# First layer of a two-layer trunk: parameter loads put ahead of four weight loads, parameters transposed 65 products earlier, one exponential on 64 values

## The chip, the cores and the metric

The kernel runs on one core of a Trainium2 chip. TensorE (PE) multiplies, VectorE (DVE), ScalarE (ACT) and GpSimd (POOL) work on tiles beside it, and SyncE (SP) issues the DMAs. The metric is the device time of one execution in microseconds, as the median of three runs. Beside it there is one profiled execution with its trace.

## What is computed

Two layers follow one another. Each projects 256 rows of 2048 columns to queries, keys, values and the input `u` of a state-space part, mixes them, multiplies by `w_out`, normalizes, and runs an MLP of 8192 columns. Cut to what matters here:

```
for l in range(2):
    proj = x @ w_in[l]                      # q, k, v, u: 1024 columns each
    attn_out = diff_attention(q, k, v, ...)  # 8 heads, softmax over allowed keys
    dt = exp(ssm_log_dt)[:, None]            # 64 groups: 64 different values
    mag = exp(lam_re * dt)                   # 64 groups x 64 states
    a   = mag * (cos(lam_im * dt), sin(lam_im * dt))
    f   = (a - 1) / lam                      # complex
    bb  = f * b                              # h[t] = a h[t-1] + bb u[t];  y = Re(c h) + d u
    ssm_out = norm(glu(gelu(y)))
    x = layer_norm(ALPHA * x + concat(attn_out, ssm_out) @ w_out[l])
    x = layer_norm(ALPHA * x + relu(x @ w_up[l])**2 @ w_down[l])
```

## The kernel before

**Products.** Every large product is made of matmuls of 128x128 by 128x512 (L202, called products below). A float32 factor is split into a high and a low part, and three products (high by high, high by low, low by high) stand for one. Weights come in tiles `w` of 256 rows by 512 columns (512 KB). For each, SP issues one DMA (L180, `wpair`), ACT copies the high part `wh` (L155), and DVE subtracts to get the low part `wl` (L136). Six tiles `w` and four pairs `wh`, `wl` can be held at once. A group of 256 rows x 512 columns of output is 96 products (16 blocks of 128 rows by 2 halves by 3). In each layer the mixer has eight such groups of the input projection: keys (first half), two of `u`, queries, two of values, keys, queries. Then 96 products with the first half of the attention output follow, which are ready early. That makes 864 products; what comes then needs the end of the state-space part or of the attention.

**State-space part.** Its parameters are loaded by `load_params`, a generator that SP's order follows: `prm` (32x128 twice), `ld` (the 64 values of `ssm_log_dt`), `vec`, `lb` (two tiles, 64-byte pieces), `lc` (c_re and c_im, two DMAs each, 256-byte pieces) and `lq` (four broadcasts). `lay_params` turns them: PE transposes `prm` and `vec` to `prmT_ps`, then `lc` in four groups of four. POOL takes two powers of e (`ex` for dt, `mag`), each 128x32. DVE makes the angles `ang`, ACT takes sine and cosine `pw`, and DVE forms `ab`, `f` and `base`. Then POOL makes `abc`, `fine` and the table `tab` (`half_prep`, `ssm_prep`). After that the part runs in eight blocks b0 to b7 of 128 channels. Each block has two groups of small matmuls `X` (L540, 8 each), which DVE multiplies with `tab`, scans, and multiplies again (tiles `wk`), and then a group `Y` (L572, L581), followed by a gelu on DVE and ACT.

**Attention.** Each of eight heads has scores `S`, a softmax on DVE and ACT (tiles `pe`), a transpose and a product `pT`, a norm with a power `ss` on POOL, and a transpose of `o`.

**What sets the order.** SP and PE run in the order in which the program emits its steps. In the mixer that order comes from `Flow`, a planner with a clock of its own (`fl.now`): each step is given a due time with constants such as `L_LOAD` and `L_PARAM`, and a step with a lower priority number is taken first once it is due. The constants only place instructions; the chip's waits are on semaphores. DVE, ACT and POOL are ordered by a scheduler from the same emission. A DMA of SP waits for the one eight places before it.

In the first layer the loop in `main` over the first product calls the parameter loads: five steps of the generator at the fourth of its steps (i == 3), and the rest at i == 16. The first four weight tiles are loaded ahead of that. In the second layer the parameters are loaded and laid out during the first layer's MLP.

Of the kernel before, what the change touches and what calls it, by code (L numbers as in the profile page):

```python
# [13 lines left out]
ALU = mybir.AluOpType  # L14
# [29 lines left out]
L_EVAC = 1.15  # L44
L_RAW = 2.9
L_GS = 3.0
L_LOAD = 10.6
L_PARAM = 7.0
L_LAY = 15.0
L_SPLIT = 1.5  # L50
L_PREP = 3.0
# [53 lines left out]
class Event:  # L105
# [3 lines left out]
    def set(self, dt):  # L109
        self.t = self.flow.now + dt  # L110
# [6 lines left out]
def trunk(ctx: ExitStack, tc: tile.TileContext, x, w_in, lambda_q1, lambda_k1, lambda_q2, lambda_k2,  # L117
# [15 lines left out]
    V, S, G, TE, SY = nc.vector, nc.scalar, nc.gpsimd, nc.tensor, nc.sync  # L133
# [33 lines left out]
    ebase = const.tile([P, 32], F32, name="ebase")  # L167
# [8 lines left out]
    def wpair(w2d, kt0, n0, extra=False, eng=None, later=False):  # L176

        with tc.high_priority(offset=4000):
            w = wst.tile([P, 2, NB], F32, tag="w", name="w")
            SY.dma_start(out=w, in_=w2d[kt0 * P:(kt0 + 2) * P, n0:n0 + NB].rearrange("(k p) n -> p k n", p=P))  # L180
            if extra:
                wh, wl = (tile4k([P, 2, NB], F32R, "wx") for _ in range(2))
            else:
                wh, wl = (wst.tile([P, 2, NB], F32R, tag=n, name=n, bufs=WB) for n in ("wh", "wl"))
            act(wh, w)
            if later:
                return (wh, wl), lambda: sub(wl, w, wh.bitcast(F32), eng)
            sub(wl, w, wh.bitcast(F32), eng)
        return wh, wl
# [122 lines left out]
    def load_params(l):  # L312
        raw = ssm.tile([96, P], F32, tag="k0", name="prm", bufs=2)
        SY.dma_start(out=raw[0:32], in_=ssm_lambda_re[l].rearrange("(q g) p -> q (g p)", g=2))
        SY.dma_start(out=raw[32:64], in_=ssm_lambda_im[l].rearrange("(q g) p -> q (g p)", g=2))
        ld = ssm.tile([96, 2], F32, tag="ld", name="ld")
        SY.dma_start(out=ld[64:96], in_=ssm_log_dt[l].rearrange("(q g) -> q g", g=2))
        vec = ssm.tile([32, P], F32, tag="k0", name="vec", bufs=2)
        for i, v in enumerate((attn_norm_g, ssm_norm_g)):
            SY.dma_start(out=vec[8 * i:8 * i + 8], in_=v[l].rearrange("(b p) -> b p", p=P))  # L320
        for j in range(LC):
            SY.dma_start(out=vec[16:32].rearrange("x (r j c) -> x r j c", r=2, j=LC)[:, :, j],
                         in_=ssm_d[l].rearrange("(x r c) -> x r c", r=2, c=32))
        yield
        lb = [ssm.tile([P, NP_, GC], F32, tag="wk", name="lb", bufs=WK) for _ in range(2)]
        for a, v in zip(lb, (ssm_b_re, ssm_b_im)):
            SY.dma_start(out=a, in_=v[l].rearrange("(q g) p c -> (g p) q c", g=2))
            yield
        lc = [tile4k([P, 8, 2, HD], F32, "lc") for _ in range(2)]
        for i, v in enumerate((ssm_c_re, ssm_c_im)):  # L330
            for g in range(2):
                SY.dma_start(out=lc[i][:, :, g], in_=v[l].rearrange("(b g) c p -> (g c) b p", g=8))
                yield
        lq = ssm.tile([P, 4, HD], F32, tag="abc", name="lq")
        for i, v in enumerate((lambda_q1, lambda_k1, lambda_q2, lambda_k2)):
            SY.dma_start(out=lq[:, i], in_=v[l].partition_broadcast(P))
        return raw, ld, vec, lq, lb, lc

    def lay_params(fl, p, l, loaded):
        raw, ld, vec, lq, lb, lc = loaded  # L340
        V.tensor_copy(out=raw[64:96].rearrange("q (g p) -> q g p", g=2),
                      in_=ld[64:96].unsqueeze(2).to_broadcast([32, 2, 64]))
        yield fl.slot("tp", dt=L_PARAM)
        give = fl.take("tp")
# [3 lines left out]
        prm = ssm.tile([P, 96], F32, tag="prmT", name="prmT")  # L348
# [6 lines left out]
        def t32(tag, n=1):  # L355
            return ssm.tile([P, n, NP_], F32, tag=tag, name=tag)

        lr, li, ldt = prm[:, 0:32], prm[:, 32:64], prm[:, 64:96]
        ex = t32("ex", 2)
        G.tensor_tensor(out=ex[:, 0], in0=ebase[:, 0:32], in1=ldt, op=ALU.pow)  # L360
        dt = ex[:, 0]
        tmp = t32("tmp", 4)
        mul(tmp[:, 0], lr, dt)
        th = t32("th")[:, 0]
# [319 lines left out]
    def turn_x(t):  # L684
        for g in range(4):
            ps = transpose4(lambda i: res[t][:, (4 * g + i) * P:(4 * g + i + 1) * P])
            xT.put(t, 4 * g, ps)
# [7 lines left out]
    loading = load_params(0)  # L695
# [159 lines left out]
    def mixer(l, p, xT, first):  # L855
# [10 lines left out]
        loaded = []  # L866
# [3 lines left out]
        def state_space():  # L870
            if l == 0:
                yield lambda: loaded
                yield fl.after(L_LOAD)
                yield from lay_params(fl, p, 0, loaded[0])
# [22 lines left out]
        def steps(g, dt=0.68):  # L897
            while True:
                try:
                    next(g)  # L900
                except StopIteration as e:
                    return e.value
                fl.now += dt
                yield lambda: True
# [12 lines left out]
        def uproj(i):  # L917
            raw = tile4k([P, 16, LC, 32], F32, "uraw")

            def turn():  # L920
                for g in range(2):
                    yield fl.slot("tp", dt=L_RAW if g == 0 else 0.0)
                    give = fl.take("tp")
                    ps = transpose4(lambda n: raw[:, 8 * g + 2 * n:8 * g + 2 * n + 2].rearrange("p r j c -> p (r j c)"))
                    fl.now += 0.44
                    act(uT[i][:, 4 * g:4 * g + 4], ps)
                    give(L_EVAC)
                    u_ev[i][g].set(L_EVAC)

            def done(j, acc):  # L930
                act(raw[:, :, j], acc.rearrange("p (x c) -> p x c", c=32))
                if j == LC - 1:
                    fl.add(0, turn())
            return project(3 * AW + i * NB, done, parity=True)

        def kproj(i):
            kT[i] = tile4k([P, 4, T], F32, "kT")
            done = lambda t, acc: fl.add(2, to_T(fl, t, acc, kT[i], k_ev[i]))
            return project(AW + i * NB, done) if i else steps(first(done))

        def qproj(i):
            qT[i] = tile4k([P, 4, T], F32, "qT")
            return project(i * NB, lambda t, acc: fl.add(2, to_T(fl, t, acc, qT[i], q_ev[i], HD ** -0.5)))
# [69 lines left out]
        def main():  # L1013
            if l == 0:
                for i, test in enumerate(kproj(0)):
                    if i == 3:
                        with tc.manual_schedule(engines={ENG.Activation, ENG.DVE}):
                            turn_x(1)
                            first_w.append(wpair(w_in[0], 6, AW))
                        fl.now += 1.76  # L1020
                        for _ in range(5):
                            next(loading)
                    if i == 16:
                        loaded.append((yield from steps(loading, 0.0)))
                        SY.dma_start(out=gb, in_=glu_b[l].partition_broadcast(P))
                    yield test
            else:
                yield from kproj(0)
            for i in range(2):
                yield from uproj(i)  # L1030
            yield from qproj(0)
            attention(0)
            yield from values(0)
            yield from values(1)
            yield from kproj(1)
            yield from qproj(1)
            attention(1)
            projected.set(0.0)
            jobs = [(g_ev, lambda i=i: glu(i)) for i in range(2)]
            seen = set()  # L1040

            def part(get, kt0, nb):
                scale = None if nb in seen else ALPHA
                seen.add(nb)
                return out_part(get(), kt0, nb, scale)

            for kt0, need, get in ((0, both(*mA_ev[0:4]), lambda: mA[0]), (4, both(*mA_ev[4:8]), lambda: mA[1]),
                                   (8, mS_ev[0], lambda: mS[0])):
                jobs += [(need, lambda a=(get, kt0, nb): part(*a)) for nb in range(4)]
            while jobs:  # L1050
                yield lambda: any(need() for need, _ in jobs)
                i = next(i for i, (need, _) in enumerate(jobs) if need())
                yield from jobs.pop(i)[1]()
            yield mS_ev[1]

        fl.add(9, main())
        fl.add(0, state_space())
        fl.add(1, glu_inputs())
# [4 lines left out]
    for l in range(DEPTH):  # L1063
# [24 lines left out]
        for f in range(1, NF):  # L1088
# [6 lines left out]
            if f == 2 and l + 1 < DEPTH:  # L1095
                loading = load_params(l + 1)
            if 2 <= f < 10 and l + 1 < DEPTH:
                try:
                    next(loading)
                except StopIteration as e:  # L1100
                    loaded = e.value
# [32 lines left out]
```

## Time and profile before

| what | us |
|---|---|
| median of 3 runs (range) | 2312.05 (2311.9 to 2314.99) |
| profiled execution, its own time | 2316.09 |
| its span, first to last instruction | 2314.4 |
| PE busy in the span | 2203.0 (95%) |
| DVE, ACT, POOL busy | 1542.6, 1076.9, 330.4 |

The profiled execution is 4.0 us above the median, and 1.7 us of its time lie outside the span. A busy share tells how much of the span an engine had an instruction in work. The rows in the section below are from the trace of this execution; times in them count from the first instruction.

### The profile page before, as it was taken

What the parts mean: (1) busy time and instruction counts of PE and PEld (TensorE: products, weight loads), DVE (VectorE), ACT (ScalarE), POOL (GpSimd) and SP (SyncE); (2) the same over time, 40 slices, a digit from 0 to 9 for tenths busy, and PEclk for the clock granted to TensorE, in tenths of its full rate; (3) what the DMA queues carried; (4) which work ended last, traced back from release to release, by engine and by line L of the source; (5) the groups of instructions that cost most, each with busy time, mean ns of one, the idle gap of its engine ahead of it and who ended that gap; (6) DMA issues with size and microseconds to landing.
All of it is one profiled execution on the core that took longest, in us unless ns stands there. A gap on an engine that the chain in (4) does not pass through costs nothing.

```text
span 2314.4 us, 29243 instructions
## 1 busy us (share of the span) xinstructions
PE 2203.0 (95%) x10772; PEld 1781.9 (77%) x10772; DVE 1542.6 (67%) x2242; ACT 1076.9 (47%) x1527; POOL 330.4 (14%) x527
## 2 busy tenths in 40 slices
PE   8888979999999999999999799899999999999997
PEld 6766757788888878788878577677888888888886
DVE  4587887865565556656677978878565555556557
ACT  3444545354444444444445454644444444444443
POOL 1766310000000001700002842000000000000001
PEclk9988989999999999999999999999999999999999
DMA  8433424566766656566755343464666666565563
GB/s 257 136 112 100 146 73 145 191 189 188 202 192 187 207 180 187 165 199 183 239 155 154 116 128 111 134 193 147 199 183 190 192 188 190 185 197 184 183 201 144
DMA packets 227055, 396.54 MB, mean 171 GB/s; under 512 B 38336, under 2 KB 38496, under 8 KB 226912
## 3 DMA queue, kind: packets, MB, share of 16 engines
q1 hardware_dynamic: 226912, 394.68, 55.3%
q8 instruction: 85, 1.39, 0.2%
q14 instruction: 58, 0.48, 0.1%
HBM read 392.53 MB, written 2.10 MB: 171 GB/s over the span
## 4 chain that ended last, share of the span: by engine, by line
PE 77%; DVE 12%; POOL 3%; issue 3%; ACT 2%; DMA 1%; SPq 1%; DVEq 0%; ACTq 0%; POOLq 0%
PE acc L202 71%; DVE wk L136 3%; DVE wl L136 3%; POOL tm L136 2%; PE tp L237 2%; PE acc L757 2%; DVE wk L554 2%; DVE res L152 1%; ACT wh L155 1%; PE Y L581 1%; DMA w<-in_w_in 1%; PE X L540 1%; DVE res L136 0%; PE pT L642 0%; DVE st L712 0%
## 5 line engine op out<-in xcount | busy, mean ns | idle before, releaser
L136 DVE TENSOR_TENSOR wl<-w,wh 128x1024 fp32r<-128x1024 f32 x714 | 882.7, 1238 | 623.6 <-ACT wh L155 611.2
L155 ACT ACTIVATE wh<-w 128x1024 fp32r<-128x1024 f32 x714 | 755.6, 1060 | 844.0 <-PE acc L202 800.1
L202 PE MATMUL acc<-wh,xTh 128*128 128x512 f32 x1440 | 569.0, 402 | 8.8 <-ACT uraw L155 6.4
L202 PE MATMUL acc<-wl,xTh 128*128 128x512 f32 x1440 | 569.2, 395 | 2.9 <-DVE wl L136 2.9
L202 PE MATMUL acc<-wh,xTl 128*128 128x512 f32 x1440 | 567.8, 395 | 0.0
L202 PE MATMUL acc<-wh,hidh 128*128 128x512 f32 x1024 | 406.2, 397 | 4.9 <-DVE res L136 4.6
L202 PE MATMUL acc<-wh,hidl 128*128 128x512 f32 x1024 | 400.3, 391 | 0.0
L202 PE MATMUL acc<-wl,hidh 128*128 128x512 f32 x1024 | 399.2, 390 | 0.0
L202 PEld LDWEIGHTS acc<-wh,xTh 128*128 128x128 f32 x1440 | 275.6, 191 | 72.8 <-ACT uraw L155 7.3
L202 PEld LDWEIGHTS acc<-wl,xTh 128*128 128x128 f32 x1440 | 275.5, 191 | 60.1 <-DVE wl L136 6.4
L202 PEld LDWEIGHTS acc<-wh,xTl 128*128 128x128 f32 x1440 | 275.1, 191 | 58.2
L202 PEld LDWEIGHTS acc<-wh,hidh 128*128 128x128 f32 x1024 | 192.8, 188 | 44.4 <-DVE res L136 5.6
L202 PEld LDWEIGHTS acc<-wh,hidl 128*128 128x128 f32 x1024 | 192.6, 188 | 41.3
L202 PEld LDWEIGHTS acc<-wl,hidh 128*128 128x128 f32 x1024 | 192.9, 188 | 38.2
L136 DVE TENSOR_TENSOR res<-res,acc 128x512 f32<-128x512 f32 x288 | 196.4, 682 | 19.0 <-PE acc L202 17.2
L285 POOL TENSOR_TENSOR rs<-rs,mhalf 128x1 f32<-128x1 f32 x8 | 7.8, 973 | 1061.1 <-DVE rs L149 1061.1
L136 POOL TENSOR_TENSOR tm<-tab,pw 128x64 f32<-128x64 f32 (+2 forms) x192 | 123.6, 664 | 177.1 <-ACT tab L155 171.0
L155 ACT ACTIVATE raw<-acc 128x512 f32<-128x512 f32 x80 | 47.0, 588 | 57.2 <-PE acc L202 57.2
L136 DVE TENSOR_TENSOR wk<-X,tab 128x128 f32<-128x128 f32 x256 | 54.4, 278 | 17.6 <-PE X L540 16.3
L432 POOL TENSOR_TENSOR lel<-ebase,lsl 128x2 f32<-128x2 f32 x2 | 1.4, 710 | 448.1 <-DVE lsl L430 448.1
L136 POOL TENSOR_TENSOR tab<-tm 128x64 f32<-128x64 f32 (+2 forms) x96 | 61.5, 641 | 6.7
L202 PE MATMUL acc<-wh,mAh 128*128 128x512 f32 x128 | 52.9, 414 | 1.8 <-DVE res L152 1.8
(179 smaller groups left out, 2026.6 us busy)
## 6 DMA issues: line engine op xcount, KB each, us to landing
w<-in_w_up SPq DMA_DIRECT2D x256, 512.0 KB, 4.1
w<-in_w_down SPq DMA_DIRECT2D x256, 512.0 KB, 5.0
w<-in_w_in SPq DMA_DIRECT2D x128, 512.0 KB, 4.4
w<-in_w_out SPq DMA_DIRECT2D x64, 512.0 KB, 3.9
w<-in_glu_w SPq DMA_DIRECT2D x16, 512.0 KB, 3.7
gb<-in_ln_g SPq DMA_DIRECT2D x8, 512.0 KB, 8.8
gb<-in_ln_b SPq DMA_DIRECT2D x8, 512.0 KB, 10.0
out<-res SPq DMA_DIRECT2D x8, 256.0 KB, 2.1
```

What stands on the lines that cost most here:

```text
L136: (eng or V).tensor_tensor(out=out, in0=in0, in1=in1, op=op)
L152: V.scalar_tensor_tensor(out=out, in0=a, scalar=s, in1=b, op0=op0, op1=op1)
L155: S.activation(out=out, in_=in_, func=func, **kw)
L202: TE.matmul(out=acc, lhsT=a[:, c], rhs=b, start=(first and i == 0), stop=(last and i == 2))
L237: TE.transpose(ps[:, i], src(i), ident)
L285: G.tensor_tensor(out=self.rs, in0=self.rs, in1=mhalf[:, 0:1], op=ALU.pow)
L432: G.tensor_tensor(out=el, in0=ebase[:, 0:2], in1=sl, op=ALU.pow)
L540: TE.matmul(out=X[:, ri], lhsT=bT[rows, 2 * ri + hf], rhs=u[rows, hf], start=True, stop=True)
L554: V.tensor_tensor_scan(out=g[:, r], data0=ml, data1=s[:, r], initial=0.0, op0=ALU.mult, op1=ALU.add)
L581: TE.matmul(out=d, lhsT=cx[:, 2 * i + ri, 2 * hf + r].rearrange("p g c -> p (g c)"), rhs=e, start=(i == 1 and ri == 0), stop=(ri == 1), sk ...
L757: TE.matmul(out=acc[t], lhsT=(lo if i == LH else hi)[:, c], rhs=(wl if i == HL else wh)[:, k % 2], start=seen[t] == 0, stop=seen[t] == 3 * ...
```

## The change

All of `load_params` is now issued at i == 3, so c_im and the four `lq` go out ahead of weight tiles five to eight. The planner's constants for the transposes are smaller. The power of e is taken of `ld` itself (32 partitions by 2 values) before it is spread and transposed, so that the transposed tile holds dt and the power on 128x32 goes. `lay_params` is shared by both layers.

```
-L_LOAD = 10.6
-L_PARAM = 7.0
+L_LOAD = 9.0
+L_PARAM = 1.5
...
     def lay_params(fl, p, l, loaded):
         raw, ld, vec, lq, lb, lc = loaded
+        G.tensor_tensor(out=ld[64:96], in0=ebase[64:96, 0:2], in1=ld[64:96], op=ALU.pow)
         V.tensor_copy(out=raw[64:96].rearrange("q (g p) -> q g p", g=2),
...
-        lr, li, ldt = prm[:, 0:32], prm[:, 32:64], prm[:, 64:96]
-        ex = t32("ex", 2)
-        G.tensor_tensor(out=ex[:, 0], in0=ebase[:, 0:32], in1=ldt, op=ALU.pow)
-        dt = ex[:, 0]
+        lr, li, dt = prm[:, 0:32], prm[:, 32:64], prm[:, 64:96]
...
                         fl.now += 1.76
-                        for _ in range(5):
-                            next(loading)
+                        loaded.append((yield from steps(loading, 0.0)))
                     if i == 16:
-                        loaded.append((yield from steps(loading, 0.0)))
                         SY.dma_start(out=gb, in_=glu_b[l].partition_broadcast(P))
```

On SP, the queue of DMAs in the first product changes as follows (- is before, + is the change; `lb`, `lc` and `lq` are parameters, `w` weight tiles):

```order
 L327 DMA lb<-in_ssm_b_im 128x32x16
 L332 DMA lc<-in_ssm_c_re 128x8x64 x2
-L180 DMA w<-in_w_in 128x2x512 x4
 L332 DMA lc<-in_ssm_c_im 128x8x64 x2
 L336 DMA lq<-in_lambda_q 128x64
```

The four tiles are put back behind the four `lq`, directly ahead of `glub`, a tile of 512 KB that stood there before.

On PE, the parameter transposes stood after the 126th product (the 30th of the second group) and now stand after the 63rd (of the first group). The later steps move with them: the first `X` of b0 to b7 stood after product 303, 375, 438, 501, 657, 723, 786 and 849, and now stands after product 243, 309, 381, 444, 597, 663, 729 and 792. The scores `S` of the heads move by at most twelve products, but for the last, which moves from 864 to 885. At the end of the 864 products, the rows of PE before were these (the second `X` of b7, then its `Y` behind three products):

```order
L540 MATMUL X<-uT,bT 128x128 x4
L635 MATMUL pT<-ident,pe 128x128 x3
L202 MATMUL acc<-wh,mAh 128x512
L202 MATMUL acc<-wl,mAh 128x512
L202 MATMUL acc<-wh,mAl 128x512
L642 MATMUL pT<-v,PT 128x128 x3
L607 MATMUL S<-kT,qT 128x128 x2
L607 MATMUL S<-kT,qT 128x256 x2
L237 MATMUL tp<-ident,o 128x128 x2
L572 MATMUL Y<-uT,k_2868 32x128 x2
```

and at the same place now (the second `X` of b7 lies 60 products and its `Y` 12 products ahead of them):

```order
L202 MATMUL acc<-wh,mAh 128x512
L202 MATMUL acc<-wl,mAh 128x512
L202 MATMUL acc<-wh,mAl 128x512
L633 MATMUL pT<-ident,pe 128x128 x3
L640 MATMUL pT<-v,PT 128x128 x3
L237 MATMUL tp<-ident,uT 128x128 x8
L605 MATMUL S<-kT,qT 128x128 x2
```

The last three products of the 864 stand there in both. What followed `Y` before, the transposes of `uT` for the gate of the state-space part, now comes directly behind the head's `pT`.

On POOL, at the start of the chain for the state-space part, the rows before were:

```order
L432 TENSOR_TENSOR lel<-ebase,lsl 128x2
L484 MEMSET k_699 128x128
L484 MEMSET k_993 128x128
L360 TENSOR_TENSOR ex<-ebase,prmT 128x32
L367 TENSOR_TENSOR mag<-ebase,tmp 128x32
L136 TENSOR_TENSOR tm<-base,ab 128x256 x2
```

and are now:

```order
L341 TENSOR_TENSOR ld<-ebase,ld 32x2
L430 TENSOR_TENSOR lel<-ebase,lsl 128x2
L482 MEMSET k_585 128x128
L482 MEMSET k_879 128x128
L365 TENSOR_TENSOR mag<-ebase,tmp 128x32
L136 TENSOR_TENSOR tm<-base,ab 128x256 x2
```

The power `ex` is gone from between the transposes and `mag`, and a smaller one stands ahead, on the loaded values.

## Rows read from the trace of the kernel before

**Rows 1.** Page, part 1: busy us (share of the span) and instructions by engine.

```profile
PE 2203.0 (95%) x10772; PEld 1781.9 (77%) x10772; DVE 1542.6 (67%) x2242; ACT 1076.9 (47%) x1527; POOL 330.4 (14%) x527
```

**Rows 2.** Windows, mixer of each layer: us, busy by engine, PEclk, DMA share, GB/s.

```profile
41.40:441.73 400.33, 355.67 (x2007) 277.14 (x2007) 311.25 (x630) 195.43 (x385) 152.14 (x246) 0.92 0.44 140
1205.80:1576.97 371.17, 337.34 (x1969) 265.43 (x1968) 296.18 (x582) 183.36 (x360) 100.19 (x168) 0.96 0.46 143
```

**Rows 3.** Timeline, SP: start, us, DMA issues (x count) in the first product.

```profile
24.89 3.44 SPq L332 DMA_DIRECT2D lc<-in_ssm_c_im  x2
28.37 3.11 SPq L336 DMA_DIRECT2D lq<-in_lambda_q  x1
33.97 0.43 SPq L1025 DMA_DIRECT2D glub<-in_glu_b  x1
```

**Rows 4.** Windows, two stretches of the DMA queue, columns as in group 2.

```profile
24.80:30.40 5.60, 5.33 (x24) 4.08 (x24) 1.54 (x2) 2.16 (x3) 0.00 (x0) 1.00 1.02 361
33.00:37.20 4.20, 4.20 (x20) 3.33 (x19) 1.09 (x1) 0.60 (x1) 0.00 (x0) 1.00 0.12 27
```

**Rows 5.** Timeline, ACT: `wh` of weight tiles 5, 8 and 9, [idle before].

```profile
27.44 1.06 ACT L155 ACTIVATE wh<-w 128x1024 fp32r<-128x1024 f32 x1 [6.31 <-DMA w<-in_w_in]
31.77 1.06 ACT L155 ACTIVATE wh<-w 128x1024 fp32r<-128x1024 f32 x1 [0.35 <-DMA w<-in_w_in]
41.27 1.06 ACT L155 ACTIVATE wh<-w 128x1024 fp32r<-128x1024 f32 x1 [5.06 <-DMA w<-in_w_in]
```

**Rows 6.** Timeline, PE: waits at products 50, 97 and 98.

```profile
29.82 0.50 PE L202 MATMUL acc<-wl,xTh 128*128 128x512 f32 x1 [0.27 <-DVE wl L136]
42.38 0.50 PE L202 MATMUL acc<-wh,xTh 128*128 128x512 f32 x1 [0.88 <-ACT wh L155]
43.64 0.63 PE L202 MATMUL acc<-wl,xTh 128*128 128x512 f32 x1 [0.76 <-DVE wl L136]
```

**Rows 7.** Windows, PE after that wait, columns as in group 2.

```profile
43.64:47.05 3.41, 3.41 (x8) 2.64 (x9) 3.07 (x3) 3.02 (x5) 0.00 (x0) 0.53 1.05 387
```

**Rows 8.** Timeline, PE and POOL: the parameter chain from transpose to table.

```profile
52.54 0.25 PE L346 MATMUL prmT_ps<-ident,prm 96*128 96x96 f32 x1
39.30 0.72 POOL L432 TENSOR_TENSOR lel<-ebase,lsl 128x2 f32<-128x2 f32 x1 [37.21 <-DVE lsl L430]
53.89 5.44 POOL L360 TENSOR_TENSOR ex<-ebase,prmT 128x32 f32<-128x32 f32 x1 [0.66 <-DVE prmT L349]
61.67 5.43 POOL L367 TENSOR_TENSOR mag<-ebase,tmp 128x32 f32<-128x32 f32 x1 [2.34 <-DVE tmp L136]
77.56 0.62 POOL L136 TENSOR_TENSOR tm<-base,ab 128x256 f32<-128x256 f32 x1 [1.36 <-DVE base L136]
109.41 0.74 POOL L136 TENSOR_TENSOR tab<-tm 128x256 f32<-128x256 f32 x1
```

**Rows 9.** Timeline, POOL: the same two multiplications twice.

```profile
91.45 2.40 POOL L136 TENSOR_TENSOR tm<-fine,pw 128x64 f32<-128x64 f32 x2
94.33 0.55 POOL L136 TENSOR_TENSOR tm<-fine,pw 128x64 f32<-128x64 f32 x2
```

**Rows 10.** Timeline, ACT and PE: the wait at product 289.

```profile
98.07 0.51 ACT L155 ACTIVATE tab<-fine 128x128 f32<-128x128 f32 x2 [6.19 <-POOL fine L136]
101.70 0.65 PE L202 MATMUL acc<-wh,xTh 128*128 128x512 f32 x1 [4.75 <-ACT uraw L155]
```

**Rows 11.** Timeline, DVE and PE: blocks b2, b3 beside the first heads.

```profile
187.89 0.67 DVE L136 TENSOR_TENSOR o<-o,ss 128x256 f32<-128x256 f32 x1 [4.17 <-POOL ss L658]
191.83 1.19 PE L540 MATMUL X<-uT,bT 64*128 64x128 f32 x6 [3.41 <-DVE ge L152]
```

**Rows 12.** Windows and timeline, PE: products 816 to 864.

```profile
300.36:352.50 52.14, 34.58 (x235) 24.89 (x233) 43.10 (x108) 22.87 (x67) 3.61 (x6) 0.79 0.19 62
305.80 0.69 PE L635 MATMUL pT<-ident,pe 128*128 128x128 f32 x2 [5.17 <-DVE pe L152]
336.51 0.65 PE L581 MATMUL Y<-wk,cx 128*32 128x128 f32 x8 [5.29 <-DVE wk L136]
```

## The prediction

> **What bounds the kernel now.** I read the page first, then windows over the mixer of each layer, then the timelines of SP, ACT, PE, POOL and DVE in the first 120 us and around the end of the first mixer. PE is busy for 95% of the span [rows 1], so a gain must come from a place where PE waits or runs at half clock. The change touches the first layer's mixer, so I compared the two layers from the end of the first key product to the first norm: 400.3 us in the first layer and 371.2 in the second [rows 2]. The reader is to see both causes. PE is idle for 44.7 us in the one and 33.8 in the other, and the granted clock is 0.92 against 0.96, which is up to 32 us against up to 15. The second layer lays its parameters out during the MLP before it. About 29 us is therefore what late parameters and late weights cost the first layer, and the ceiling for this change.
>
> **A. Weight tiles five to eight go behind c_im and lq: a loss.** Before, the copy of tile 5 began at 27.44 and that of tile 8 at 31.77, 1.44 us apart [rows 5]. c_im was issued at 24.89, the first lq was taken at 28.37 and held SP for 3.11 us, and glub followed at 33.97 [rows 3]. Tile 9, right behind glub, was copied at 41.27 [rows 5]. Now tile 5 stands where glub stood. Ahead of it the four tiles are missing, which filled the queue from 24.80 to 30.40 (361 GB/s for 5.60 us are their 2 MB) [rows 4]. So its copy begins at 41.27 - 1.44 - 5.60 = 34.2. From a copy's start to the product that needs `wl`, PE took 43.64 - 41.27 = 2.4 us at tile 9 [rows 5, 6], so product 50 runs at 36.6 instead of 29.82 [rows 6]: 6.8 us late. Nothing covers it, since products 49 to 96 all need these tiles. Behind the wait at 42.38 the granted clock was 0.53 for 3.41 us [rows 7], so nearly all of that stretch was at 1.2 GHz and 1.6 us were lost; I charge the same here. A is +8.4. From below: while the four lq went, the queue was nearly empty for 4.2 us (share 0.12) [rows 4]; if tile 5 slips in there, A is +4.2. From above: one more stretch at half clock, +10. I take 8.4, since SP issues in order and the lq are still ahead.
>
> **B. The wait at products 97 and 98 goes.** It was 0.88 + 0.76 us [rows 6] and its half clock 1.6. Products 50 to 96 took from 29.82 to 41.5 (42.38 less its wait), 0.24 us each with a few transposes. Now the group ends near 36.6 + 11.7 + 1.6 + about 1.5 for the 16 transposes of lc that now lie inside it = 51.4, long after tile 9. B is -3.2, and falls only where A falls too.
>
> **C. The parameter chain comes earlier.** The transposes follow 14 products after 36.6: eight at half clock (3.4 us), six at 0.24, so 41.5 instead of 52.54 [rows 8], 11.0 earlier. The power `ex` goes: from its start at 53.89 to that of `mag` at 61.67 are 7.8 us [rows 8]. The new power has 32x2 values; the nearest row is `lel`, 128x2, 0.72 us [rows 8]. It runs on loaded values before the wait of A and is hidden by it; uncovered it would cost those 0.7 us. In the second layer all of it lies under the MLP. Against this, the second sine now stands on ACT behind copies that need the end of the first group (51.4), and four subtractions of weights stand on DVE ahead of `ab`. I take 5 us back. POOL then begins its multiplications with the full `base` at 77.56 - 11.0 - 7.8 + 5 = 63.8, and the table of b0, done at 110.2 [rows 8], is done at 96.4. PE is at the second X of b0 (after product 255) at 51.4 + 159 x 0.24 + about 3.5 of small matmuls = 93.1, and needs the slots that DVE empties some 0.8 us after the table: a wait of 4.1, with 1.6 of half clock. In exchange the wait at 101.70 goes: PE waited 4.75 for `uraw`, which stood on ACT behind a copy that waited 6.19 for POOL's `fine` [rows 10]; `fine` now comes 13.8 us earlier and PE is later. That is 6.4 with its half clock. C is 5.7 - 6.4 = -0.7. Bounds: -6.4 where no wait takes its place, +4 where the chain is as late as it was without `ex`.
>
> Something in the trace speaks against C. POOL's pair of multiplications on 128x64 took 0.55 us once and 2.40 us three microseconds earlier [rows 9], 1.85 more, beside subtractions of weights on DVE. The moved chain has about ten such subtractions beside it where it had eight; two more meetings would make C +3.0. I leave that out of the sum, since the pairs meet by chance of the moment. The Trainium skill, GPSIMD Engine Reference, section Specifications, says that GpSimd shares its SBUF interfaces with VectorE and meets contention with instructions of two SBUF inputs; this pair of rows agrees.
>
> **D. Blocks b2 and b3 beside the first heads.** At 187.89 DVE had waited 4.17 for the power `ss`, queued on POOL behind the preparation of b4; PE then waited 3.41 at an X of b3 for the gelu behind it [rows 11]. Now the Y of b3 lies 117 products behind its second X, and POOL is a block further when `ss` comes. I take -4: this wait and a part of its half clock. From below nothing, because the softmax of the first head now meets b2 where it met b1; from above -10.
>
> **E. The end of the 864 products.** From 300.36 to 352.50, PE was busy for 34.6 of 52.1 us at a clock of 0.79 [rows 12]: 17.6 idle, up to 10.9 in clock. The longest waits are at a pT, 5.17, and at the last Y, 5.29, both for DVE [rows 12]. Between the second X of b7 and its Y stood three products. Now 48 lie there, and the 45 further ones (10.8 us) are more than the 5.29 that were missing; DVE also has one block less to do in this stretch. The wait at Y goes, so does most of what follows it, and about half of the clock's share; the wait at pT stays. I take -12. From below 0, if DVE (43.1 of 52.1 busy) sets the pace anyway; from above -22.
>
> **The sum.** 8.4 - 3.2 - 0.7 - 4 - 12 = -11.5. The profiled execution took 2316.09 in all (span 2314.4 and 1.7 around it), so 2304.6; the median of the runs is 4.0 lower, so **2300.5**.
>
> **The rivals.**
> 1. *Slower.* The waits of D and E belong to DVE's work and not to the order, and A stands at +10: DVE was 83% busy in the last stretch [rows 12], and its work is not less. Then +6.1, 2318. It decides when D and E together give less than 4.5. Against it: DVE is idle for 89 of 400 us of this mixer, and the second layer, with the same work, needs 29 less [rows 2].
> 2. *About the same.* E gives half, D nothing: -1.5, 2310.5. For it: what moves by 60 products meets other heads, and new waits appear where none were.
> 3. *Contention on POOL.* Two meetings more at 1.85 us [rows 9] put C at +3.0: -7.8, 2304. The chain lies earlier all the same, so this moves the time and not the sign. The rule of GPSIMD Engine Reference speaks for it.
> 4. *Faster than forecast: the weights are not late*, because tile 5 uses the empty stretch of the queue; then A is 4.2, and D and E reach -8 and -14: about -21, 2291. That the loads were hidden anyway is part of this case.
>
> **How the numbers follow.** Forecast 0.42, rival 1 0.16, rival 2 0.20, rival 3 0.10, rival 4 0.12. 0.2% (4.6 us) is about what a measurement of this kernel can tell from no change. Faster by more: the forecast, rival 4 and nearly all of rival 3, 0.63; within it 0.21; slower 0.16. The likeliest case alone spans 2295 to 2306, by D and E. The range leaves out rival 1 and the far end of rival 4: 2288 to 2314.
>
> **What the changed profile would show.** A: PE idle from about 29.2, the copy of tile 5 on ACT near 34.2, product 50 near 36.6, a low clock for 3 to 4 us. B: no wait at the first product of `u`. C: prmT near 41.5, no `ex`, the table of b0 near 96, a wait at the second X of b0 and none near product 289. E: the last Y without a long wait, and windows of the last 80 products with less than 10 us idle. The first norm, at 441.7, should come 8 to 16 us earlier, and all behind it be moved by that and otherwise unchanged. The forecast is wrong if the copy of tile 5 comes after 37, if the table comes after 100, or if the new order of blocks and heads puts waits of some microseconds between products 300 and 800 where none were.

## The result, and the profile after

The median fell from 2313.52 us (four runs, 2311.9 to 2315.47) to 2297.65 (four runs, 2295.69 to 2299.01): the ratio is 0.9931, with a 95% interval of 0.9915 to 0.9947, so 15.9 us less. The forecast of 2300.5 was reckoned from the 2312.05 of three of these runs. The profiled execution took 2297.46; its span is 2295.7.

Windows of the first and the second mixer, in the order of columns of [rows 2]; each runs, as there, from the end of its first key product to its first norm:

```profile
52.93:426.35 373.42, 340.79 (x1989) 265.98 (x1988) 305.09 (x604) 188.87 (x379) 149.55 (x242) 0.96 0.46 144
1188.97:1558.35 369.38, 336.05 (x1969) 264.31 (x1968) 296.33 (x583) 183.43 (x360) 100.35 (x168) 0.96 0.47 144
```

In this stretch the first layer took 400.3 us and now takes 373.4, near the 369.4 of the second layer. But the first key product ends 11 us later. Its place in the timelines of SP, ACT and PE (compare [rows 3, 5, 6]):

```profile
22.45 1.84 SPq L332 DMA_DIRECT2D lc<-in_ssm_c_im  x2
24.33 1.15 SPq L336 DMA_DIRECT2D lq<-in_lambda_q  x1
26.95 3.92 SPq L180 DMA_DIRECT2D w<-in_w_in  x4
30.92 0.93 SPq L1021 DMA_DIRECT2D glub<-in_glu_b  x1
34.45 1.06 ACT L155 ACTIVATE wh<-w 128x1024 fp32r<-128x1024 f32 x1 [12.54 <-DMA w<-in_w_in]
35.56 0.80 PE L202 MATMUL acc<-wh,xTh 128*128 128x512 f32 x1 [5.42 <-ACT wh L155]
36.82 0.79 PE L202 MATMUL acc<-wl,xTh 128*128 128x512 f32 x1 [0.46 <-DVE wl L136]
```

Tile 5 is issued at 26.95 and copied at 34.45; PE waits 5.42 + 0.46 us for it. From that product on (columns of [rows 2]) the granted clock was 0.50, that is 1.2 GHz, up to 42.49; it had fallen at 32.25, while PE was waiting:

```profile
35.56:42.49 6.93, 6.47 (x14) 4.74 (x15) 4.88 (x4) 3.17 (x3) 0.00 (x0) 0.50 1.05 393
```

The parameter chain on POOL, with a row of DVE between, and the second `X` of b0 on PE (compare [rows 8, 9]):

```profile
17.11 0.94 POOL L341 TENSOR_TENSOR ld<-ebase,ld 32x2 f32<-32x2 f32 x1 [15.03 <-DMA ld<-in_ssm_log_dt]
44.95 5.43 POOL L365 TENSOR_TENSOR mag<-ebase,tmp 128x32 f32<-128x32 f32 x1 [1.51 <-DVE tmp L136]
64.55 0.62 POOL L136 TENSOR_TENSOR tm<-base,ab 128x256 f32<-128x256 f32 x1 [1.96 <-DVE base L136]
79.21 2.46 DVE L136 TENSOR_TENSOR wl<-w,wh 128x1024 fp32r<-128x1024 f32 x2 [4.65 <-ACT wh L155]
79.29 2.54 POOL L136 TENSOR_TENSOR tm<-fine,pw 128x64 f32<-128x64 f32 x2
82.30 0.56 POOL L136 TENSOR_TENSOR tm<-fine,pw 128x64 f32<-128x64 f32 x2
98.24 0.72 POOL L136 TENSOR_TENSOR tab<-tm 128x256 f32<-128x256 f32 x1
99.74 1.68 PE L538 MATMUL X<-uT,bT 64*128 64x128 f32 x8 [3.83 <-DVE wk L136]
```

The table of b0 is done at 98.96 instead of 110.15, and PE waits for it all the same. Later in the mixer these are the longest waits of PE in its timeline (the second compares with [rows 12]):

```profile
171.23 0.45 PE L633 MATMUL pT<-ident,pe 128*128 128x128 f32 x1 [5.22 <-DVE pe L152]
305.20 0.62 PE L633 MATMUL pT<-ident,pe 128*128 128x128 f32 x2 [3.22 <-DVE pe L152]
```

The first of them, at the first head, was shorter before the change:

```profile
157.96 0.69 PE L635 MATMUL pT<-ident,pe 128*128 128x128 f32 x2 [2.06 <-DVE pe L152]
```

The window from the last of the 864 products to the first product with the gate, `gSh`, of after and then of before, columns of [rows 2]:

```profile
321.66:333.38 11.72, 7.43 (x53) 5.28 (x51) 8.77 (x19) 9.37 (x27) 0.89 (x2) 0.97 0.31 93
```

```profile
324.99:352.50 27.51, 15.12 (x109) 10.01 (x107) 20.73 (x56) 13.19 (x42) 2.71 (x4) 0.73 0.12 39
```

The 27.5 us with PE busy for 15.1 have become 11.7 with 7.4, and the granted clock in them has risen from 0.73 to 0.97. Where the difference between the two executions grows and shrinks is read by counting the products in the two timelines of PE and comparing the start of the same product (each timeline has 8640 products):

| product | before | after | later by |
|---|---|---|---|
| 0 | 9.91 | 10.77 | +0.9 |
| 48 | 29.16 | 35.56 | +6.4 |
| 96 | 42.38 | 52.93 | +10.6 |
| 150 | 60.34 | 66.06 | +5.7 |
| 260 | 89.03 | 103.65 | +14.6 |
| 289 | 102.15 | 111.57 | +9.4 |
| 375 | 135.85 | 143.58 | +7.7 |
| 540 | 207.21 | 205.19 | -2.0 |
| 810 | 297.97 | 300.34 | +2.4 |
| 863 | 324.75 | 321.43 | -3.3 |
| 870 | 355.23 | 336.07 | -19.2 |
| first norm | 441.73 | 426.35 | -15.4 |

The changed kernel is behind for most of the mixer, and 15.9 us appear between products 863 and 870. But small matmuls were moved too and now stand between other products, so a difference between two rows of this table holds moved work as well as waits. Idle time (the window less PE's busy time) and the clock tell the two apart. Windows from product 0 to the first norm, then of products 150 to 289, 289 to 810, and 810 to the first norm, before and then after, columns of [rows 2]:

```profile
9.91:441.73 431.82, 384.44 (x2122) 298.69 (x2123) 325.82 (x649) 206.54 (x399) 152.86 (x247) 0.93 0.47 146
60.34:102.15 41.81, 35.38 (x168) 28.35 (x167) 23.76 (x41) 20.39 (x36) 28.61 (x45) 1.00 0.48 140
102.15:297.97 195.82, 178.11 (x1110) 135.70 (x1109) 157.39 (x341) 97.61 (x212) 113.21 (x191) 0.91 0.39 119
297.97:441.73 143.76, 124.87 (x655) 99.14 (x654) 117.03 (x228) 67.03 (x125) 4.50 (x8) 0.92 0.46 150
```

```profile
10.77:426.35 415.58, 373.66 (x2122) 291.00 (x2123) 328.84 (x649) 204.51 (x399) 157.04 (x247) 0.95 0.49 151
66.06:111.57 45.51, 39.41 (x205) 31.64 (x203) 25.37 (x40) 20.25 (x38) 39.76 (x70) 0.96 0.41 129
111.57:300.34 188.77, 171.63 (x1150) 129.97 (x1149) 163.95 (x356) 96.18 (x209) 100.59 (x162) 0.95 0.40 123
300.34:426.35 126.01, 116.62 (x579) 93.39 (x578) 103.11 (x187) 64.13 (x122) 6.24 (x8) 0.97 0.54 171
```

All stretches between product 0 and the first norm whose granted clock was 0.50, added up (eleven of them before, seven after), before and then after:

```profile
sum 61.47, PE 48.79 PEld 36.54 DVE 39.41 ACT 25.02 POOL 32.16; mean PE 4.44 PEld 3.32 DVE 3.58 ACT 2.27 POOL 2.92
```

```profile
sum 37.54, PE 27.89 PEld 20.97 DVE 24.62 ACT 12.74 POOL 16.36; mean PE 3.98 PEld 3.00 DVE 3.52 ACT 1.82 POOL 2.34
```

PE ran the same 2122 matmuls in both. Its idle time fell from 47.4 to 41.9 us. Half of what PE was busy at the low clock is lost to it: 24.4 us before, 13.9 after. What is left, 360.0 and 359.7 us, is the same. So of the 16.2 us by which this stretch became shorter, 5.5 are idle time and 10.5 are clock.

### The profile page after: what moved, and what is told of

The parts are those of the page before. It is cut to its first block, busy times and chain, and to the rows that moved or that the text cites. A ratio compares the mean times of both kernels' runs of the same rounds, so it can differ in the third digit from the quotient of the medians.

```text
span 2295.7 us, 29249 instructions
## 1 busy us (share of the span) xinstructions
PE 2189.3 (95%) x10772; PEld 1772.1 (77%) x10772; DVE 1545.6 (67%) x2242; ACT 1075.2 (47%) x1527; POOL 328.2 (14%) x527
## 4 chain that ended last, share of the span: by engine, by line
PE 73%; DVE 15%; issue 4%; POOL 3%; ACT 2%; DMA 1%; SPq 1%; DVEq 0%; ACTq 0%; POOLq 0%
PE acc L202 67%; DVE wk L136 4%; DVE wl L136 3%; DVE wk L552 2%; POOL tm L136 2%; PE acc L755 2%; PE tp L237 2%; DVE res L152 1%; ACT wh L155 1%; DMA w<-in_w_in 1%; PE Y L579 1%; DVE res L136 0%; PE X L538 0%; DVE st L710 0%; POOL abc L136 0%
## 5 line engine op out<-in xcount | busy, mean ns | idle before, releaser
L136 POOL TENSOR_TENSOR tm<-tab,pw 128x64 f32<-128x64 f32 (+2 forms) x192 | 130.3, 699 | 156.8 <-ACT tab L155 150.6
L552 DVE TENSOR_TENSOR_SCAN wk<-magL,wk 128x128 f32<-128x128 f32 x128 | 55.4, 502 | 0.0
```

The source lines that it names most:

```text
L136: (eng or V).tensor_tensor(out=out, in0=in0, in1=in1, op=op)
L552: V.tensor_tensor_scan(out=g[:, r], data0=ml, data1=s[:, r], initial=0.0, op0=ALU.mult, op1=ALU.add)
```

## Experiments

Three things were changed at once: the place of the loads, the power, and two numbers that move instructions on PE. Each can be undone alone, because `L_LOAD` and `L_LAY` can put PE's order back, instruction by instruction, to that of before or of the change. "Old order" and "new order" below mean this. The transposes moved from product 126 to 63, by 63 products (the title says 65). All times, each with its ratio to the kernel before on the same chip:

| kernel | loads | power | blocks on PE | median | ratio (95%) |
|---|---|---|---|---|---|
| before | late | 128x32 | old | 2313.4 | 1 |
| loads_only | early | 128x32 | old | 2321.60 | 1.0033 (1.0021 to 1.0045) |
| loads_only_again | early | 128x32 | old | 2320.17 | 1.0026 (1.0016 to 1.0036) |
| pow_only | late | 32x2 | old | 2308.27 | 0.9979 (0.9970 to 0.9988) |
| loads_and_pow | early | 32x2 | old | 2313.89 | 1.0002 (0.9993 to 1.0011) |
| weights_first_late | late | 32x2 | old, transposes new | 2306.58 | 0.9969 (0.9958 to 0.9981) |
| late_blocks | early | 32x2 | old, transposes new | 2309.12 | 0.9979 (0.9970 to 0.9987) |
| constants_only | late | 128x32 | new | 2298.90 | 0.9937 (0.9925 to 0.9950) |
| ex_back | early | 128x32 | new | 2302.13 | 0.9950 (0.9938 to 0.9963) |
| weights_first | late | 32x2 | new | 2294.93 | 0.9919 (0.9905 to 0.9932) |
| weights_first_again | late | 32x2 | new | 2296.66 | 0.9926 (0.9914 to 0.9938) |
| the change | early | 32x2 | new | 2297.65 | 0.9931 (0.9915 to 0.9947) |
| weights_first_mid | late | 32x2 | new, blocks 9 products later | 2297.59 | 0.9935 (0.9921 to 0.9948) |
| weights_first_p | late | 32x2 | new, heads' `pT` later | 2305.44 | 0.9962 (0.9948 to 0.9976) |

In the traces, PE was idle between product 810 and the first norm for 18.9 to 20.4 us in the seven kernels with the blocks in the old order, and for 9.0 to 10.5 in the five with the new one.

**loads_only.** Against before, the old order on PE:

```
-L_LOAD = 10.6
+L_LOAD = 19.4
...
-                        for _ in range(5):
-                            next(loading)
                     if i == 16:
-                        loaded.append((yield from steps(loading, 0.0)))
```

with the full `load_params` at i == 3, as in the change.

> The kernel before with one edit: all parameter loads go out at the fourth step, so c_im and the four lq stand ahead of weight tiles 5 to 8. L_LOAD is raised so that on TensorE every instruction stands where it stood before (transposes behind product 126). This is term A and B alone. Theory: product 50 runs near 36.8 as in the changed kernel (7.0 late), the wait at products 97 and 98 goes, about 5 us remain at the first norm, 2316 to 2320 us. Rival: PE waits for DVE and the parameter chain later in the mixer anyway and makes the loss good there: 2313 to 2315, no difference to before.

It was 8.2 us slower than before by the medians. Timeline of PE at product 48:

```profile
35.44 0.80 PE L202 MATMUL acc<-wh,xTh 128*128 128x512 f32 x1 [6.37 <-ACT wh L155]
```

So the loads alone lose time, and in the old order nothing later makes it good; the rival falls. The time lies above the theory's range too; the last two runs below go back to it.

**pow_only.** The part of the diff in `lay_params` alone, against before.

> The kernel before with one edit: the power of e is taken of ld (32x2) and ex (128x32) goes; loads and planner constants as before, and on TensorE the same order. This is the part of term C that needs no new order. Theory: mag starts near 54 instead of 61.67, the table of b0 comes about 7 us earlier, and the wait of 4.75 us at 101.70 with its half clock goes: 6 us faster, 2306 to 2309. Rival: DVE sets the pace at the first heads (products 390 to 500), and what PE gains at 101.70 it waits there: less than 2 us of gain, 2311 to 2314.

It gained 5.1 us. `mag` came at 53.43 instead of 61.67, 8.2 earlier, but the table of b0 only 3.7 earlier. Timelines of POOL and PE:

```profile
53.43 5.44 POOL L365 TENSOR_TENSOR mag<-ebase,tmp 128x32 f32<-128x32 f32 x1 [1.75 <-DVE tmp L136]
70.49 1.53 POOL L136 TENSOR_TENSOR tm<-base,ab 128x256 f32<-128x256 f32 x1 [11.62 <-DVE base L136]
105.69 0.72 POOL L136 TENSOR_TENSOR tab<-tm 128x256 f32<-128x256 f32 x1
96.32 0.50 PE L202 MATMUL acc<-wh,xTh 128*128 128x512 f32 x1 [1.28 <-ACT uraw L155]
107.19 1.81 PE L538 MATMUL X<-uT,bT 64*128 64x128 f32 x8 [2.64 <-DVE wk L136]
```

POOL waited 11.62 us for `base`, where it had waited 7.98 before: DVE and ACT now end last there. The wait at product 288 shrank from 4.75 [rows 10] to 1.28, and one of 2.64 came at an `X`. The gain was a little less than the theory's 6 us, inside its range, and the rival falls.

**weights_first**, and once more **weights_first_again.** Against the change:

```
-L_LOAD = 9.0
+L_LOAD = 0.4
...
-                        loaded.append((yield from steps(loading, 0.0)))
+                        for _ in range(5):
+                            next(loading)
                     if i == 16:
+                        loaded.append((yield from steps(loading, 0.0)))
```

> The changed kernel with the loads in the old order: five steps of the parameter loads at the fourth step and the rest at i == 16, so weight tiles 5 to 8 go ahead of c_im and lq. L_LOAD is 0.4 so that on TensorE every instruction stands where it stands in the changed kernel. Theory: the wait of 5.42 us for tile 5 goes, the one at products 97 and 98 comes back, and 5 us of the 8.4 - 3.2 are gained: 2291 to 2294. Rival: PE comes 7 us earlier to the second X of b0, and the parameter chain does not come as much earlier, so the wait there of 3.83 us grows by what was gained: 2296 to 2299, as the changed kernel.

> The kernel with the weights first once more, unchanged, to have its distance from the changed kernel (2297.65) from more runs. By the traces it is 6.8 us ahead at the last of the 864 products and 3.2 ahead at the first norm. Theory: 2293.5 to 2295.5, so that the early loads cost 2 to 4 us in the new order. Rival: no difference from the changed kernel, 2296.5 to 2298.

2294.93, above the theory's range and below the rival's, and 2296.66, in the rival's. The intervals of both overlap that of the change, so the two runs together, some 2 us below it, do not show a difference. In the first trace PE was 6.8 us ahead of the change at the last of the 864 products and 3.2 ahead at the first norm (423.13 against 426.35); between them it waited 2.56 us for `PT` at an unchanged place, where the change waited 1.36. In the second trace, of the same kernel, it was 3.1 ahead and then 2.5, and waited 1.85. So a lead of some us at product 864 differs from one execution to the next, and a part of it is lost behind. The wait at the second `X` did not grow, against the rival:

```profile
93.79 1.67 PE L538 MATMUL X<-uT,bT 64*128 64x128 f32 x8 [3.85 <-DVE wk L136]
```

The whole chain moved with the weights.

**late_blocks.** One number against the change, which restores the old order from the first `X` on:

```
-L_LAY = 15.0
+L_LAY = 40
```

> The changed kernel with one number changed: L_LAY 40 instead of 15. The loads, the transposes behind product 63 and the power on 64 values stay; the eight blocks, the heads and the end of the 864 products stand on TensorE exactly where they stood before the change. Theory (terms D and E): the gain comes from the place of the blocks, above all from the last Y and the gate, which again stand behind product 864; 16 us are lost there, about 5 us (the wait at the second X of b0 with its half clock) come back: 2306 to 2312. Rival: the gain comes from the parameters being ready earlier, whatever the order, and the time stays at 2296 to 2300.

2309.12, 11.5 us slower than the change. The window from the last of the 864 products to the gate's, and from the timeline of PE the last `Y`:

```profile
321.83:349.68 27.85, 14.73 (x107) 9.84 (x106) 20.98 (x56) 12.87 (x43) 2.71 (x4) 0.75 0.13 38
```

```profile
333.59 0.65 PE L579 MATMUL Y<-wk,cx 128*32 128x128 f32 x8 [5.52 <-DVE wk L136]
```

PE reaches the last of the 864 products within half a us of the change (321.83 and 321.43), and then the 27.9 us of before are back. This is what shows that the place of the blocks carries the gain. The theory holds, and the rival, that earlier parameters carry it, falls.

**weights_first_late.** `L_LAY = 40` in weights_first.

> The kernel with the weights first (loads in the old order, transposes behind product 63, power on 64 values) with L_LAY 40: blocks and heads stand on TensorE where they stood before the change. Against the kernel with the power alone (2308.3) only the transposes lie earlier. Theory: three waits at products 288, 315 and 369 (1.28, 2.64 and 1.91 us, of which the last is for wk and may stay) go, and the place of the blocks still costs some 8 to 11 us against the weights-first kernel: 2302 to 2306. Rival: earlier transposes are worth nothing where blocks do not move: 2307 to 2309.

2306.58: between the theory's range and the rival's, and its interval overlaps that of pow_only, so with late loads the earlier transposes alone show no gain. The one number cost 11.7 us against the first run of weights_first (9.9 against the second, 11.5 in the pair above).

**ex_back.** The power on 128x32 put back into the change.

> The changed kernel with the power put back where it was: ex on 128x32 behind the transposes, no power on ld. Loads, constants and the order on TensorE as in the changed kernel. Theory: mag starts 8 us later (in the kernel with the power alone it came 8.2 earlier), the table of b0 3.7 to 7 us later, and the wait of 3.83 us at the second X of b0 grows by that; nothing later makes it good: 2301 to 2305. Rival: DVE sets the pace from the first head on, and what is lost at the second X is made good at the waits for the first head and at the end: 2297 to 2299.

**constants_only.** Against before, two numbers and nothing else:

```
-L_LOAD = 10.6
-L_PARAM = 7.0
+L_LOAD = 0.4
+L_PARAM = 1.5
```

> The kernel before with two numbers changed, L_LOAD 0.4 and L_PARAM 1.5: loads in the old order, ex as before, but every instruction on TensorE stands where it stands in the changed kernel. Theory: the order of the blocks on TensorE carries the gain, and against the kernel with the weights first, at 2294.9, only the missing power shows, 4 to 7 us: 2299 to 2302, 11 to 14 us faster than before. Rival: the new order pays only with a parameter chain that is as early as it, and without the power the wait at the second X of b0 takes most of it: 2306 or more.

ex_back took 2302.13, inside the theory's range, and constants_only 2298.90, 0.1 us below it; both rivals fall. The second `X` of b0 in the timelines of PE, ex_back and then constants_only:

```profile
101.97 1.81 PE L540 MATMUL X<-uT,bT 64*128 64x128 f32 x8 [9.67 <-DVE wk L136]
```

```profile
100.42 1.81 PE L540 MATMUL X<-uT,bT 64*128 64x128 f32 x8 [9.88 <-DVE wk L136]
```

Without the small power this wait is 6 us longer than the 3.83 of the change. In the total that is 4.5 us (ex_back against the change), or 2.2 to 4.0 (constants_only against the two runs of weights_first). Yet constants_only, whose loads and power are those of before, is as fast as the whole change to within the intervals. By the medians the loads' loss and the power's gain cancel.

**weights_first_mid.** `L_LAY = 28` in weights_first.

> The kernel with the weights first and L_LAY 28: the first X of b0 stands behind product 252 instead of 243, the later blocks 9 products later each, and the last Y behind product 864 instead of 852, ahead of the scores of the next head. Theory: the wait of 3.85 us at the second X of b0 shrinks by 9 x 0.24 = 2.2 us, but the last Y falls behind the 864 products, and 3 to 6 us of the gain at the end go: 2295 to 2300. Rival: the end does not hang on the place of the last Y, and the time is 2292 to 2294.

2297.59, inside the theory's range, and not told apart from weights_first. The wait at the second `X` went, and the one at the first head, 5.08 us in weights_first, became longer:

```profile
159.13 0.66 PE L633 MATMUL pT<-ident,pe 128*128 128x128 f32 x2 [7.33 <-DVE pe L152]
```

The last `Y` stands behind product 864 here, as before the change, but 48 products behind the second `X` of b7 instead of 3. PE was idle for 10.1 us from product 810 to the first norm, as in the new order (10.5 and 10.3 in weights_first), and not for the 19.6 of weights_first_late. So the idle time at the end does not hang on the place of `Y` behind product 864; it goes with the room between `X` and `Y`, or with how early the block begins, which no run separates.

**weights_first_p.** `L_P = 11.2` instead of 9.6 in weights_first.

> The kernel with the weights first (2294.9) and L_P 11.2 instead of 9.6: a head's transposes pT stand up to 15 products further behind its scores, from the second head on; the blocks move by at most three products. Theory: PE waits there for the softmax on DVE (3.60 us at product 816, 5.08 at 438), the wait at 816 shrinks by its six products, 1.4 us, that at 438 by its three, 0.7, and the time is 2291 to 2294. Rival: DVE sets the pace of this stretch, the wait turns up at the next place that needs DVE, and the time is 2294 to 2297.

2305.44: both theory and rival are wrong, it lost 8.8 to 10.5 us against the two runs of weights_first. At product 959 it was only 1.9 behind weights_first; the first norm came 11.7 later (434.85 against 423.13). Windows of behind that product, of this kernel and then of weights_first:

```profile
359.00:372.00 13.00, 6.73 (x25) 5.17 (x26) 12.29 (x32) 6.80 (x17) 1.17 (x2) 0.69 0.27 84
```

```profile
355.00:368.00 13.00, 11.28 (x50) 8.64 (x49) 12.88 (x27) 6.69 (x9) 0.00 (x0) 1.00 0.43 130
```

DVE is busy for 95% of the first and 99% of the second; PE was left with nothing that did not need DVE in the first. The later `pT` put the end of the last head behind product 960, ahead of the next products, and PE waited 2.44, 1.73 and 1.90 us there.

**loads_only_again** and **loads_and_pow.** The first is loads_only unchanged; the second is pow_only with the early loads and `L_LOAD = 19.4`.

> The kernel with the loads alone once more, unchanged. It was 8.2 us above before by the medians, while its trace is 3.9 us behind before at the last of the 864 products and 3.3 behind at the end, and the same loads cost 2.7 and 3.2 us in the two pairs with the new order. Theory: the loads cost 3 to 5 us here too and the first measurement stood high: 2316.5 to 2319. Rival: with the transposes behind product 126 the loads cost 8 us, and it comes out at 2320 to 2322 again.

> The kernel with the power alone (2308.3), with the early loads added and the order on TensorE of before. Theory: the loads cost 3 to 5 us: 2311 to 2313.5. Rival: with the transposes behind product 126 they cost 8 us: 2315.5 to 2317.

2320.17 is 6.9 us above before, in the rival's range. 2313.89 is 5.6 above pow_only, above the theory's range and below the rival's. The theory of 3 to 5 us falls, and the rival's 8 is at the upper end of what the three runs show. With the transposes behind product 126 the early loads cost 5.6 to 8.2 us. With the transposes behind product 63 they cost less: 3.2 (ex_back against constants_only), 2.5 (late_blocks against weights_first_late) and 1 to 2.7 (the change against the two runs of weights_first). Each of these last pairs has intervals that overlap; that all have the same sign is what speaks for a cost. A row of weights_first, from the timeline of PE, shows a part of the difference:

```profile
37.41 0.66 PE L237 MATMUL tp<-ident,lc 128*128 128x128 f32 x4 [2.71 <-DVE vecT L352]
```

There PE, with its weights in time, comes to the transposes of `lc` too early and waits 2.71 us behind product 69. Where the weights are late this wait is gone, and from product 60 to 96 PE of the change made up 3.8 of the 10.0 us by which it was behind weights_first (5.5 of 10.0 against the second trace). With the transposes behind product 126 no such wait stands there to be saved. By medians the early transposes are worth 4.8 us with early loads (late_blocks against loads_and_pow, intervals apart) and with late ones nothing that shows.

## Why the prediction was right

Forecast 2300.5, measured 2297.65; the likeliest case (the forecast, not a rival) is the one that came. The gain was forecast at 11.5 us and measured at 15.9; the times lie closer than that because the kernel before has since measured 2313.52 instead of 2312.05. By the prediction's own steps, with the half clock reckoned as half of PE's busy time at 0.50:

- **A** (+8.4) had its places right: copy of tile 5 at 34.45 (34.2), product 50 near 36.8 (36.6). Its half clock was mis-sized: 6.47 us of PE's work lay in it, so 3.2 were lost and 1.6 charged. **B** (-3.2): the wait at products 97 and 98 is gone. Together, less the 0.9 us that the executions differ at product 0, they are +4.9 at product 150 (5.2 forecast); with A's clock as it was, that closeness is in part luck. In the total the loads cost 1 to 3 us with the new order and 5.6 to 8.2 with the old transposes.
- **C** (-0.7) came out: `prmT` at 42.75 (41.5), the table done at 98.96 (96.4), a wait of 3.83 at the second `X` (4.1), none at product 289. From product 150 to 289 the kernel fell back by 3.7 us, but mostly because PE has 205 matmuls there instead of 168: the `X` of b0 and transposes, which stood behind product 289 before. Idle time in the stretch went from 6.4 to 6.1, and the one stretch at half clock costs 1.7 in both (before, it lay mostly behind product 289): C was -0.3. The chain from POOL's multiplications with the full `base` to the table took 34.4 us where it had taken 32.6. Rival 3's contention was there: the pair at 79.29 took 2.54 us while DVE's two subtractions ran from 79.21 for 2.46, and the next pair 0.56. The Trainium skill's GPSIMD Engine Reference, section Specifications, names such contention, and this trace agrees.
- **D** (-4) was mis-sized, and by its waits it would have been nothing. The 3.41 us at the `X` of b3 went, but the wait at the first head's `pT`, where the softmax met b2 as the lower bound of D had it, grew from 2.06 to 5.22; this is a wait of the kind that the prediction named as a sign of being wrong. Idle time from product 289 to 810 is 17.7 us before and 17.1 after. What fell is the half clock: 13.4 us without the 1.6 that belong to C, and 5.8 after. So D was -8.2, and nearly all of it is clock. Why the clock fell less often there, with as much idle time, was not worked out. The 117 products between the second `X` of b3 and its `Y`, which D named, were 114 before, so they are no reason.
- **E** (-12) had the mechanism right and the size near. From product 810 to the first norm idle time fell from 18.9 to 9.4 us and the half clock from 7.6 to 3.2: E was -13.9. (By the table the difference falls by 17.7 there, because PE has 579 matmuls in it instead of 655.) The long wait at the last `Y` went, and most of what follows it, as the step had it: in the old order `Y`, the gelu and the transposes for the gate stood behind waits of 3.54 and 5.29 us with no product beside them.

The start, A with B, C, D and E, 0.9 + 4.9 - 0.3 - 8.2 - 13.9, are -16.6. The first norm came 15.4 earlier; against the sum stand 1.2 us more of PE's busy time at full clock behind product 150, of 317, which I do not assign. So D was too small by 4.2 us and E by 1.9, and these are what the forecast of 11.5 lacked, less the 0.9 and the 1.2.

That the remainder would be unchanged did not hold quite: the profiled executions differ by 18.6, so 3.3 us come after the first norm. By the same count of products 1.6 of them come between products 3000 and 4000, in the first layer's MLP, where the second layer's parameters are transposed (at product 3204), and most of the rest in the second mixer (371.2 and 369.4 by the windows). The first part is there, at 1.5 to 1.6 us, in the trace of every kernel with the small power and in none with the old one but ex_back, so the power alone is not shown as its cause. The median changed by 15.9, near the 15.4, and the profiled execution of before lies 2.6 above its median, so part may be the spread of executions.

Rival 1 gave the sign wrong but named a true thing: DVE holds PE up at the end. Of a lead of 6.8 us, 3.6 were lost there in one execution of weights_first (0.6 of 3.1 in the other), and a wait moved there cost some 10 us (weights_first_p). That the order helps by giving PE products that do not need DVE while DVE works is how I read late_blocks and weights_first_mid together; no run moves the last block alone.

What the prediction did not see is how the change divides. Two numbers give nearly the whole gain (14.5 of 15.9 us by the medians); loads and power cancel. "Parameters earlier" pays through the places that the planner gives to the blocks, not through the earlier data.

## What to carry to other kernels

When two engines alternate, look at what stands behind the last independent work of a phase: a chain that must still run there leaves PE idle, and moving the blocks earlier by some 60 products was worth 10 to 12 us here where no wait at the old place was longer than 5.5. Count the clock with the waits: of what this change saved up to the first norm, two thirds was PE's work at the low clock and one third idle time. Before believing in a change with several parts, put each part's order back with the planner's constants and time it alone: here one part lost what another gained. And the price of a delay depends on the waits around it: by the medians the same late weights cost some three times as much where no other wait stood beside them.

## What was not expected of the hardware

- The same c_im and first lq held SP for 3.44 and 3.11 us behind four weight tiles [rows 3], and for 1.84 and 1.15 ahead of them. While the first lq held SP, the DMAs moved 361 GB/s before and 227 after.
- The power of e took 0.94 us on 32x2 and 5.43 on 128x32; 0.72 on 128x2 [rows 8]. In these rows it goes by the elements of a partition.
- A pair of POOL multiplications lasted nearly as long as the two DVE subtractions beside it (2.54 and 2.46 us), against 0.56 three us later: the rows look as if it stood until they were over.
